# Sums of the softmax by two products with a matrix of ones, in place of transposes and a row sum, in a Hymba encoder block

## The chip, the cores and the metric

The kernel runs on one core of a Trainium2 chip. The metric is the device time in microseconds. The engines are TensorE (PE; PEld is its weight load), VectorE (DVE), ScalarE (ACT), GpSimd (POOL) and SyncE (SP), which issues most of the DMAs. Each engine works through its own instructions in a fixed order and waits on semaphores for the others.

## The reference

One encoder block: 2048 tokens and 16 meta tokens of width 1024, four query heads that share two key/value heads of width 128, four Fourier groups, and an MLP of width 4096, all in float32. The part that the change touches is the softmax of the attention:

```python
h = concat([meta, x])                               # (2064, 1024)
proj = rms_norm(h, g_mix) @ w_in                    # q, k, v, u
q, k = (axial_rope(rms_norm(t, g)) for t, g in ((q, g_q), (k, g_k)))
s = einsum('bkgqd,bksd->bkgqs', q, k) / sqrt(128)
p = softmax(s, axis=-1)
attn = einsum('bkgqs,bksd->bkgqd', p, v)
four = real(fft2(u over tokens and channels)) @ w_f
h = h + concat([rms_norm(attn), rms_norm(four)]) @ w_out
h = h + square(relu(rms_norm(h) @ w_up)) @ w_down
out = rms_norm(h, g_final)[16:]
```

## The kernel before

Products of float32 that have to be exact are taken in two parts: `split` (L67) has ScalarE round a value to float32r, the high part, and VectorE subtract it from the value, the low part; `mm3` (L77) adds three products of such parts. Lines L70/L71 and L80 to L82 are therefore those of many operations, and the tiles' names tell them apart.

The kernel runs in stages: projections with rotary embedding (to about 340 us in the profile), then attention with other work beside it (to about 990 us), then the MLP, by Strassen's scheme with seven products, in two passes over the tokens.

**Attention** (`attention`, L729) runs in 16 units. A unit is 256 query tokens of one key/value group: two heads, so 512 columns. Its keys come in 16 tiles of 128 and one of 96 rows that holds the meta tokens. Scores stand transposed, with keys on the partitions and the 512 query columns along the free dimension:

- `scores` (L759): `mm3` gives a tile of scores in PSUM (tile `s`, two buffers), ScalarE copies it to SBUF (L780), and VectorE keeps a running maximum M over the tiles (L783, L786).
- `stats` (L806): the maximum over all keys of a column has to be taken across partitions. `over_keys` (L790) transposes M in four 128x128 pieces on TensorE (L794) into PSUM and VectorE reduces along the free dimension (L796); `rows_to_cols` (L799) brings the 128x4 result back to a row of 512 on all partitions by four more transposes of a broadcast column (L803). ScalarE copies it to `mb` (L811).
- `softmax` (L813): VectorE subtracts `mb` from two key tiles at once (L840), ScalarE takes the exponential (L841), VectorE adds it to a running sum `acc` (L845, L847), and TensorE multiplies it with V into the PSUM tile `o` (L849). At a unit's last tile VectorE folds `acc` to `sum` (L827, L828), 128x512.
- `finish` (L851), in three steps between which other work may stand: ScalarE copies `o` to SBUF (O, L855); then the sums over the keys, again across partitions: four transposes of `sum` (tile `pm_l`, L794), a reduction (tile `mx_l`, L796) and a reciprocal of 128x4 (L859); then four transposes back (tile `pd_l`, L803) and VectorE's multiplication of O with them, out of PSUM (L861). O is split into `ohl` (one buffer) and stored by SP (L870), or, in the last two units, split straight into the operand `at`. ScalarE squares O (L872), and VectorE adds the squares to `sq` (L876, L879).

The small PSUM tiles of these steps (`pm`, `pd`, and `pys` of the output stage) share one buffer, named "misc".

**What sets the order.** `attention` is a generator, and two others run beside it: `fourier` (tiles `pa`, `py`, `thi`, `C`, `EV`, `UA`) and `out_f` (tiles `yh`, `ysq`, `pof`, `xo`), and after these `out_a` and `flip` (tiles `poa`, `pmt`, `h`). `mix` (L1000) ties the steps of attention to theirs. A unit's finish is put into a list at its last key tile and takes one step at each of the following tiles, while the next unit's scores and exponentials go on; scores run some 20 tiles ahead of the softmax. The language's own scheduler then lays out each engine's instructions in an order of its own, with the buffers that it has, so that a change in one place may move others.

## Time and profile before

| | us |
|---|---|
| median of 3 runs | 2296.43 |
| lowest and highest | 2295.06, 2297.25 |
| profiled execution | 2295.14 |
| its span | 2293.4 |
| TensorE busy, granted clock | 2242.5, 0.994 |
| VectorE busy | 1692.7 |
| ScalarE busy | 1177.4 |
| GpSimd busy | 247.2 |

In the profile's rows a group has its line, engine and operation, the tiles it writes and reads, the shapes and a count; then the busy time in microseconds and the mean of one in nanoseconds; then the idle time before it and what ended that. A row of the timeline begins with the start and the duration in microseconds. A row of stretches has, for each engine, the busy time and the number of instructions between two times, then the granted TensorE clock, the busy share of the DMA engines and their GB/s. Instructions overlap at their ends: an engine starts the next while the last one drains, so the step from start to start is shorter than the duration.

### The profile page before, as it was taken

To read this page: it belongs to the slowest core of one execution; us is meant where nothing else is said; L and a number is where in the kernel's file an instruction comes from. 1 tells how busy PE (TensorE), PEld (TensorE's weight loads), DVE (VectorE), ACT (ScalarE), POOL (GpSimd) and SP (SyncE) were. 2 spreads that over 40 slices of the span, in tenths; PEclk is the share of its full clock that TensorE was granted. 3 is DMA by queue.
4 is the path that set the end of the run, shared out by engine and by line. 5 is a ranking of instruction groups with operands and counts; after the bars stand their busy time and mean duration, and the time that the engine had idled before them with its cause. 6 is when DMAs were issued, how large, how long until landed. Compare 5 with 4: busy or idle time off the path is not lost.

```text
span 2293.4 us, 28136 instructions
## 1 busy us (share of the span) xinstructions
PE 2242.5 (98%) x10238; PEld 1775.1 (77%) x10238; DVE 1692.7 (74%) x2250; ACT 1177.4 (51%) x1997; POOL 247.2 (11%) x285
## 2 busy tenths in 40 slices
PE   9999999999999999999999999999789999899998
PEld 7888986766666666678888878888678888688887
DVE  6435589999998998887776579779555656596795
ACT  6443356656555666677555544334345555443343
POOL 2212120013222022010000010000200000100000
PEclk9999999999999999999999999999899999999999
DMA  6333252133343523366767675543574445764442
GB/s 204 87 105 87 66 164 71 51 120 100 115 137 120 204 87 119 123 262 234 237 227 234 235 276 176 172 129 119 198 302 151 154 149 187 299 201 158 129 138 83
DMA packets 191787, 367.41 MB, mean 160 GB/s; under 512 B 15760, under 2 KB 74768, under 8 KB 189984
## 3 DMA queue, kind: packets, MB, share of 16 engines
q1 hardware_dynamic: 171040, 310.08, 39.9%
q0 software_dynamic: 20464, 55.27, 7.7%
q8 instruction: 80, 1.31, 0.2%
q14 instruction: 59, 0.48, 0.1%
q10 hardware_dynamic: 144, 0.26, 0.0%
HBM read 236.28 MB, written 129.27 MB: 159 GB/s over the span
## 4 chain that ended last, share of the span: by engine, by line
PE 79%; DVE 8%; DMA 6%; ACT 3%; issue 2%; POOL 1%; SPq 1%; POOLq 0%; DVEq 0%; ACTq 0%
PE o L849 6%; PE dx L80 5%; PE dx L82 5%; PE dx L81 5%; PE dy L82 4%; PE dy L80 4%; PE dy L81 4%; PE ux L80 4%; PE ux L81 4%; PE ux L82 4%; PE uy L80 3%; PE uy L82 3%; PE uy L81 3%; PE s L80 2%; PE s L82 2%
## 5 line engine op out<-in xcount | busy, mean ns | idle before, releaser
L70 ACT CAST ah<-a 128x1024 fp32r<-128x1024 f32 x112 | 117.1, 1049 | 259.3 <-PE dx L81 104.9
L849 PE MATMUL o<-S,vn 128*128 128x512 f32 x512 | 243.6, 597 | 4.1 <-ACT S L841 3.4
L80 PE MATMUL dx<-bh,ah 128*128 128x512 f32 x512 | 199.3, 389 | 4.2 <-DVE hs L1485 2.5
L81 PE MATMUL dx<-bl,ah 128*128 128x512 f32 x512 | 199.1, 389 | 1.4 <-DVE bl L71 1.4
L82 PE MATMUL dx<-bh,al 128*128 128x512 f32 x512 | 199.2, 389 | 0.1
L80 PE MATMUL ux<-bf,wuh 128*128 128x512 f32 x448 | 176.8, 395 | 18.8 <-DMA bf<-f_d 18.7
L780 ACT COPY S<-s 128x512 f32<-128x512 f32 x256 | 145.0, 584 | 92.2 <-PE s L82 73.0
L81 PE MATMUL ux<-bf,wuh 128*128 128x512 f32 x448 | 175.8, 392 | 0.0
L82 PE MATMUL ux<-bf,wul 128*128 128x512 f32 x448 | 175.7, 392 | 0.0
L840 DVE TENSOR_TENSOR S<-S,mb 128x1024 f32<-128x1024 f32 x128 | 155.4, 1229 | 11.8 <-ACT mb L811 11.7
L841 ACT ACTIVATE S<-S 128x1024 f32<-128x1024 f32 x128 | 135.1, 1063 | 43.1 <-DVE S L840 41.9
L80 PE MATMUL dy<-bh,ah 128*128 128x512 f32 (+1 forms) x388 | 151.6, 391 | 4.9 <-ACT ah L70 4.9
L71 DVE TENSOR_TENSOR al<-a,ah 128x1024 fp32r<-128x1024 f32 x112 | 136.3, 1222 | 26.6 <-ACT ah L70 26.0
L82 PE MATMUL dy<-bh,al 128*128 128x512 f32 (+1 forms) x388 | 150.8, 390 | 0.7 <-DVE al L71 0.7
L81 PE MATMUL dy<-bl,ah 128*128 128x512 f32 (+1 forms) x388 | 151.3, 390 | 0.0
L849 PEld LDWEIGHTS o<-S,vn 128*128 128x128 f32 x512 | 92.2, 189 | 75.0 <-issue 59.0
L80 PE MATMUL s<-q,kt 128*128 128x512 f32 (+1 forms) x272 | 145.2, 534 | 2.7 <-ACT S L780 2.5
L71 DVE TENSOR_TENSOR bl<-d,bh 128x1024 fp32r<-128x1024 f32 x96 | 117.1, 1220 | 26.7 <-ACT bh L70 26.5
L80 PE MATMUL uy<-bf,wuh 128*128 128x512 f32 x320 | 125.2, 391 | 0.3 <-ACT wuh L70 0.3
L82 PE MATMUL uy<-bf,wul 128*128 128x512 f32 x320 | 124.7, 390 | 0.7 <-DVE wul L71 0.7
L81 PE MATMUL uy<-bf,wuh 128*128 128x512 f32 x320 | 124.9, 390 | 0.0
L786 DVE TENSOR_TENSOR M<-M,S 128x1024 f32<-128x1024 f32 x96 | 117.8, 1227 | 9.1 <-ACT S L780 8.1
(311 smaller groups left out, 5633.5 us busy)
## 6 DMA issues: line engine op xcount, KB each, us to landing
a<-s_d SPq DMA_DIRECT2D x84, 512.0 KB, 3.7
R<-in_w_up_dram SPq DMA_DIRECT2D x32, 1024.0 KB, 5.5
s_d<-s SPq DMA_DIRECT2D x128, 256.0 KB, 2.1
d<-in_w_down_dram SPq DMA_DIRECT2D x52, 512.0 KB, 5.1
s_d<-c SPq DMA_DIRECT2D x96, 256.0 KB, 2.8
f_d<-lf SPq DMA_DIRECT2D x56, 256.0 KB, 2.9
bf<-f_d SPq DMA_DIRECT2D x7, 2048.0 KB, 22.6
a<-s_d POOLq DMA_DIRECT2D x24, 512.0 KB, 5.6
```

The source lines that it names most:

```text
L70: self.high = nc.scalar.copy(hi, src)
L71: self.low = nc.vector.tensor_tensor(lo, src, f32v(hi), op=ALU.subtract)
L80: nc.tensor.matmul(out, a[0], b[0], start=first, stop=False, skip_group_check=chain)
L81: nc.tensor.matmul(out, a[0], b[1], start=False, stop=False, skip_group_check=chain)
L82: nc.tensor.matmul(out, a[1], b[0], start=False, stop=last, skip_group_check=chain)
L780: nc.scalar.copy(S[:, i % 2], ps)
L786: nc.vector.tensor_tensor(M, M, S, op=ALU.max)
L840: nc.vector.tensor_tensor(S, S, mb, op=ALU.subtract)
L841: nc.scalar.activation(p, S, AF.Exp, scale=ISQ)
L849: nc.tensor.matmul(s["O"], v[:, 2 * j % 4 + e], p[:, e], start=i + e == 1, stop=False)
```

## The change

A float32r matrix of ones, 128x128, is made at the start by ScalarE. In `finish`, the `sum` tile (128x512, sums over the keys that lie on a partition) is split into two float32r parts, and two products with the ones add them over the partitions. The result, 128x512 in PSUM, has the column's sum on every partition. VectorE takes the reciprocal of all of it back into `sum`, and multiplies O by that. The transposes, the reduction and the 128x4 tiles of the sums are gone from `finish`; those of the maximum in `stats` stay as they are.

```diff
     ones = const.tile([P, 1], F32, name="ones", tag="ones")
     nc.vector.memset(ones, 1.0)
+    ones_r = const.tile([P, P], R32, name="ones_r")
+    nc.scalar.copy(ones_r, bc(ones, [P, P]))
...
             O = ap2.tile([P, 512], F32, name=f"O_{u}", tag="Osb", bufs=1)
             nc.scalar.copy(O, s["O"])
-            yield
-            sl = over_keys(s["sum"], f"l{u}", ALU.add)
-            rl = ap2.tile([P, 4], F32, name=f"rl_{u}", tag="rl", bufs=2)
-            nc.vector.reciprocal(rl, sl)
-            yield
-            nc.vector.tensor_tensor(O, O, rows_to_cols(rl, f"l{u}"), op=ALU.mult)
+            parts = ap2.tile([P, 2, 512], R32, name=f"sp_{u}", tag="ohl", bufs=1)
+            split(parts[:, 0], parts[:, 1], s["sum"])
+            yield
+            ps = misc(f"pl_{u}")
+            for e in range(2):
+                nc.tensor.matmul(ps, ones_r, parts[:, e], start=e == 0, stop=e == 1)
+            yield
+            nc.vector.reciprocal(s["sum"], ps)
+            nc.vector.tensor_tensor(O, O, s["sum"], op=ALU.mult)
             c = slice(b % 2 * 256, b % 2 * 256 + 256)
```

Line numbers after the change are larger, by two from the new constant on and by five behind `finish`.

The scheduler's new order at the first unit's finish, on VectorE. `M` and `S` with high numbers are the maximum and the scores of the next units, `mb` the maximum of the running one, `acc` its sum. Before:

```order
L783 TENSOR_TENSOR M_4001<-S_0_3929,S_2_3981 128x1024
L796 TENSOR_REDUCE mx_l_3988<-pm_l_3983 128x4
L840 TENSOR_TENSOR S_2_3745<-S_2_3745,mb_3931 128x1024
L859 RECIPROCAL rl_3990<-mx_l_3988 128x4
L786 TENSOR_TENSOR M_4001<-M_4001,S_4_4023 128x1024
L861 TENSOR_TENSOR O_3975<-O_3975,pd_l_4003 128x512
L845 TENSOR_TENSOR acc_3992<-S_0_3734,S_2_3745 128x1024
L71 TENSOR_TENSOR ohl_4009<-O_3975,ohl_4009 128x512
```

And in the changed program, at the same place (`sp` are the two parts, `pl` the product with ones):

```order
L785 TENSOR_TENSOR M_4000<-S_0_3931,S_2_3986 128x1024
L71 TENSOR_TENSOR sp_3979<-sum_3973,sp_3979 128x512
L842 TENSOR_TENSOR S_2_3747<-S_2_3747,mb_3933 128x1024
L865 RECIPROCAL sum_3973<-pl_3988 128x512
L788 TENSOR_TENSOR M_4000<-M_4000,S_4_4018 128x1024
L866 TENSOR_TENSOR O_3977<-O_3977,sum_3973 128x512
L847 TENSOR_TENSOR acc_3991<-S_0_3736,S_2_3747 128x1024
L71 TENSOR_TENSOR ohl_4004<-O_3977,ohl_4004 128x512
```

The split's low part stands where the reduction stood, the wide reciprocal where the narrow one did, and the rest is as it was; in front of the maximum, the running sum and the multiplication there is now the reciprocal of 512 columns.

On TensorE, around the same finish (`pa` belongs to the Fourier work, `o_3727` and then `o_3993` are this unit's and the next one's products with V). Before:

```order
L567 MATMUL pa_1_4087<-cw_342,EV 128x128 x4
L794 MATMUL pm_l_3983<-ident,sum_3971 128x128 x4
L829 MATMUL o_3727<-ph_16_3968,vm_3584 128x512
L567 MATMUL pa_2_4096<-cw_342,EV 128x128 x4
L567 MATMUL pa_3_4105<-cw_342,EV 128x128
L849 MATMUL o_3993<-S_0_3734,vn_0_3576 128x512 x2
L803 MATMUL pd_l_4003<-ident,rl_3990 128x128 x4
L567 MATMUL pa_3_4105<-cw_342,EV 128x128 x2
L849 MATMUL o_3993<-S_2_3745,vn_0_3576 128x512 x2
```

And in the changed program:

```order
L831 MATMUL o_3729<-ph_16_3970,vm_3586 128x512
L569 MATMUL pa_2_4091<-cw_344,EV 128x128
L863 MATMUL pl_3988<-sp_3979,ones_r 128x512
L569 MATMUL pa_2_4091<-cw_344,EV 128x128
L569 MATMUL pa_3_4100<-cw_344,EV 128x128 x2
L851 MATMUL o_3992<-S_0_3736,vn_0_3578 128x512
L863 MATMUL pl_3988<-sp_3979,ones_r 128x512
L851 MATMUL o_3992<-S_0_3736,vn_0_3578 128x512
```

The two groups of four transposes are gone; the first product with ones follows the unit's last product with V, and the second, which needs the low part, comes four rows later, between two products with V of the next unit.

## The prediction

> **What bounds the kernel now.** I read the page first (its head, its table of busy time, the slices, the chain's shares), then the busy times of the attention stage in three stretches, then the timeline around single finishes.

> ```profile
> span 2293.4 us, 28136 instructions
> PE 2242.5 (98%) x10238; PEld 1775.1 (77%) x10238; DVE 1692.7 (74%) x2250; ACT 1177.4 (51%) x1997; POOL 247.2 (11%) x285
> DVE  6435589999998998887776579779555656596795
> PE 79%; DVE 8%; DMA 6%; ACT 3%; issue 2%; POOL 1%; SPq 1%; POOLq 0%; DVEq 0%; ACTq 0%
> ```

> Over the whole span TensorE sets the time: 98% busy, 79% of the chain. But the 74% of VectorE is a mean over unlike stages. Its digits stand at 8 and 9 from the sixth slice to the eighteenth (57 us each), and that is attention. The stretches, and behind the dots the same three for the reciprocal alone:

> ```profile
> core 0: us, PE busy (x) PEld busy (x) DVE busy (x) ACT busy (x) POOL busy (x), PEclk, DMA share, GB/s
> 380.00:620.00 240.00, 235.26 (x1030) 161.34 (x1029) 235.39 (x288) 149.26 (x251) 44.27 (x42) 1.00 0.29 90
> 620.00:820.00 200.00, 199.41 (x783) 137.88 (x782) 181.55 (x229) 116.58 (x196) 42.41 (x42) 1.00 0.43 144
> 820.00:990.00 170.00, 167.30 (x672) 112.49 (x671) 144.22 (x182) 106.89 (x175) 32.91 (x23) 1.00 0.35 115
> ...
> 380.00:620.00 240.00, 1.01 (x6) 1.00 0.29 90
> 620.00:820.00 200.00, 0.84 (x5) 1.00 0.43 144
> 820.00:990.00 170.00, 0.87 (x5) 1.00 0.35 115
> ```

> Its counts (x6, x5, x5) tell how many of the 16 units finish in each stretch. In the first, VectorE works 235.39 of 240 us and so has 4.6 us left; in the second 18.5, in the third 25.8. TensorE is as dense there. So the stage has two engines at their limit, VectorE above all in its first 240 us, and both sides of the change have to be priced: what TensorE is spared and what VectorE is given.

> **What TensorE is spared.**

> ```profile
> 379.65 0.39 PE L81 MATMUL s<-q,kt 128*128 128x512 f32 x1
> 379.88 0.40 PE L82 MATMUL s<-q,kt 128*128 128x512 f32 x1
> 381.45 0.60 PE L794 MATMUL pm_l<-ident,sum 128*128 128x128 f32 x4
> 385.05 0.60 PE L803 MATMUL pd_l<-ident,rl 128*128 128x128 f32 x4
> ```

> Matmuls overlap, so what one costs is its step from start to start, not its duration. A score product of 128x512 follows the last after 379.88 - 379.65 = 0.23 us. Four transposes last 0.60 us together, of which the last alone is 0.27, so a step is (0.60 - 0.27) / 3 = 0.11. A finish loses 8 x 0.11 = 0.88 us and gains two products of the scores' shape and type, 0.46: 0.42 us less, 6.7 us over 16 units. That is the whole gain on TensorE, 0.3% of the span. The transposes of the maximum (pm_m, pd_m) stay.

> **What VectorE and ScalarE are given.** The words of the change name a row sum that VectorE loses. It gets the low part of the split in its place, of the same width, and its reciprocal grows from 128x4 to 128x512, since the sums now stand on all partitions.

> ```profile
> L859 DVE RECIPROCAL rl<-mx_l 128x4 f32<-128x4 f32 x16 | 2.7, 170 | 0.0
> L796 DVE TENSOR_REDUCE mx_l<-pm_l 128x4 f32<-128x512 f32 x16 | 10.9, 683 | 0.2 <-PE pm_l L794 0.2
> L71 DVE TENSOR_TENSOR ohl<-O,ohl 128x512 fp32r<-128x512 f32 x14 | 9.6, 687 | 0.2 <-ACT ohl L70 0.2
> L861 DVE TENSOR_TENSOR O<-O,pd_l 128x512 f32<-128x512 f32 x16 | 10.9, 681 | 1.1 <-PE pd_l L803 0.9
> L70 ACT CAST ohl<-O 128x512 fp32r<-128x512 f32 x14 | 8.7, 619 | 6.0 <-DVE O L861 6.0
> ```

> The new low part (the shape of L71) costs what the reduction did, 0.69 against 0.68 us: they cancel. The multiplication stays, with one operand now from SBUF and no longer from PSUM; L71 there, all from SBUF, lasts as long. ScalarE gets one cast of 0.62 us in each unit, 9.9 in all; it is busy 149 of 240 us in the tightest stretch, so as work this is hidden.

> What is left is the reciprocal, whose width of 512 no row shows. Here again the step counts:

> ```profile
> 384.40 0.17 DVE L859 RECIPROCAL rl<-mx_l 128x4 f32<-128x4 f32 x1
> 384.49 1.20 DVE L786 TENSOR_TENSOR M<-M,S 128x1024 f32<-128x1024 f32 x1
> ...
> 420.54 0.17 DVE L859 RECIPROCAL rl<-mx_l 128x4 f32<-128x4 f32 x1
> 420.62 1.20 DVE L783 TENSOR_TENSOR M<-S,S 128x1024 f32<-128x1024 f32 x1
> ...
> 422.88 0.68 DVE L861 TENSOR_TENSOR O<-O,pd_l 128x512 f32<-128x512 f32 x1
> 423.48 1.22 DVE L786 TENSOR_TENSOR M<-M,S 128x1024 f32<-128x1024 f32 x1
> 424.62 0.69 DVE L71 TENSOR_TENSOR ohl<-O,ohl 128x512 fp32r<-128x512 f32 x1
> ...
> 785.58 0.15 DVE L1045 COPY ass<-pas 128x4 f32<-128x4 f32 x1
> 785.65 1.40 DVE L74 SCALAR_TENSOR_TENSOR wol<-wor,cols,woh 128x512 fp32r<-128x512 f32 x2
> ```

> 512 elements step 0.60 us, 1024 step 1.14: 1.05 ns for an element and 0.06 us for the instruction. The copy of four elements fits that (0.07). The reciprocal of four elements doesn't: its successor starts after 0.09 and 0.08 us, 0.085 in the mean, 0.025 over the 0.06. Spread over four elements that is 6 ns each, six times an ordinary element. At width 512: 0.06 + 512 x 0.006 = 3.1 us.

> The ends: if what exceeds is a fixed delay of this operation, 512 elements cost what any other operation of that width does, 0.60. If 0.09 is the true reading, 0.03 over four elements is 7.5 ns, and the instruction costs 3.9. I take 3.1, since the rows show the operation itself to be slow and the excess grows with nothing else that I can name; four elements read to 0.01 us are a weak lever, so I keep both ends.

> [...]

> Per unit, then, VectorE pays 3.1 - 0.085 = 3.0 us more, 48 us over the stage.

> **What of it is on the path.** First stretch: 235.4 + 6 x 3.0 = 253.4 us of work where 240 stood. What VectorE idles there now, 4.6 us, are short waits for ScalarE and TensorE, which a longer queue doesn't remove; I leave them: 258, or **+18**. TensorE's six savings are lost in it, since it now waits. Second: 181.6 + 15 = 196.6 of 200, or 98.3% busy, as full as the first stretch is today (98.1%), and that one kept TensorE at 98%: it fits. Third: 144.2 + 15 = 159.2 of 170: it fits. In these two TensorE keeps its savings, 10 x 0.42 = **-4**. But the reciprocal is one block in an in-order queue: the subtraction, the running sum and the maximum of the next unit stand behind it for 3 us, and so do ScalarE's exponentials, which wait for the subtraction.

> ```profile
> ACT S L780 <- PE s L82: 63.5, 51, 4.6
> ACT ohl L70 <- DVE O L861: 6.0, 4, 2.2
> ```

> ScalarE now waits for O at its cast to ohl in four finishes of 16, up to 2.2 us. With O 3 us later it will wait at most of them, and behind that cast stand the copies (L780) that free the two PSUM buffers of the scores. ScalarE has time to make up for it (it idles 63.5 us for scores), the two buffers have not. TensorE's own new wait, of its second product for the low part, takes the place of its transposes' waits for the sum and for the reciprocal; the next unit's products with V stand behind it. For all of this I put half a microsecond on each of the ten finishes: **+5**.

> Last unit, in the same timeline:

> ```profile
> 986.61 0.66 PE L794 MATMUL pm_l<-ident,sum 128*128 128x128 f32 x4 [0.30 <-DVE sum L828]
> 989.08 0.69 DVE L861 TENSOR_TENSOR O<-O,pd_l 128x512 f32<-128x512 f32 x1 [0.88 <-PE pd_l L803]
> 992.70 0.89 DVE L879 TENSOR_TENSOR sq<-sq,O 128x256 f32<-128x256 f32 x2 [0.71 <-ACT O L872]
> 994.41 0.97 PEld L1042 LDWEIGHTS pas<-ones,sq 128*128 128x128 f32 x8
> ```

> From the sum to the multiplication it takes 989.08 - 986.61 = 2.5 us; then a cast of 0.62, a subtraction of 0.69, products of 0.5 and a reciprocal of 3.1, 4.9: 2.4 later. The squares end at 993.6 and the next block's product with them starts at 994.41, so 0.8 us of it is covered: **+2**.

> At no cost: the cast to ones_r at the start. ScalarE's table load ends near 2.0 us and it waits for x until 4.31, where 0.3 us of a 128x128 cast finds room; its price without that cover is that 0.3.

> ```profile
> 0.74 1.28 ACT L259 ACT_TABLE_LOAD   x1 [0.74 <-PEq L1709]
> 4.31 0.60 ACT L259 ACTIVATE jk<-x 128x512 f32<-128x512 f32 x1 [2.29 <-DMA x<-in_x_dram]
> ```

> Also the parts' use of the ohl buffer (its last store was issued a whole unit, some 38 us, earlier), and the stores of o_d that SP now issues behind some weight loads: what reads them comes several units later. The loads of keys and values on POOL change places with additions of squares, on an engine busy 11% of the span.

> Sum: 18 - 4 + 5 + 2 = +21 us on the profiled execution's 2295.14 (its span is 2293.4; 1.7 lie around it). That execution is 1.3 below the median of 2296.43, so I forecast **2316**.

> **The rivals.** *The reciprocal streams like any other operation* (0.60 us). Then VectorE pays 0.5 us a unit. The first stretch takes 235.4 + 3.1 = 238.5 of its 240 us and loses something between 0 and the 3.1, say 1, TensorE saves 4 in the others, the last unit is even (0.62 + 0.69 + 0.5 + 0.6 = 2.4): 2295 - 3 = 2292. For it: the instruction after the short reciprocal lasts 1.20 and not 1.22, so part of the delay may be handed back. Against it: the step of 0.085. It decides up to about 0.085 + 4.6 / 6 = 0.85 us for a reciprocal; above that the first stretch overflows. This is the case that is not slower.

> *Slower still* (3.9 us, 3.8 more a unit): first stretch 235.4 + 22.9 + 4.6 = 263, +23; second 200.5 of 200 with its short waits, +4; blocks and last unit +10; savings -2: +35, 2330. For it: the reading 0.09.

> *The slack is shared out.* VectorE's total from 380 to 990 is 561 us, with 48 more 609 of 610. Attention steps are tied to the steps of the Fourier and output work beside them, but each engine's order is laid out anew, so work beside attention can slip from the first stretch into the later ones. Perfectly shared, only the last unit's +2 remains: 2297. Against it: none of the three stretches now runs VectorE over 98.1%.

> **How the numbers follow.** The forecast's case 0.52 (its own range 2305 to 2326), the slower one 0.20, the streaming one 0.18, the shared slack 0.10. This kernel's measurement can tell about 0.2%, 4.6 us, from no change. Slower: 0.52 + 0.20 = 0.72. The streaming case lies at the edge of that bound: 0.10 of it within, 0.08 faster; with the shared slack, 0.20 within. The range takes in the ends of the reciprocal: 2291 to 2334.

> **What would show it.** In the changed kernel's groups, the row of the reciprocal: near 3.1 us each, 50 us in all, or 0.7. VectorE's busy share from 380 to 620 at 98% or more with fewer units finished in it, and TensorE's below 95%, waiting for VectorE's subtraction through ScalarE's exponential. ScalarE's wait for O at ohl in most finishes. If the reciprocal is short and the time still grows, the order laid out anew is the cause, not the price; if it is long and the time doesn't grow, the slack was shared.

## The result, and the profile after

| | before | after |
|---|---|---|
| median of 4 runs each, taken in turn, us | 2296.81 | 2321.81 |
| lowest and highest | 2295.06, 2297.25 | 2318.47, 2327.26 |
| ratio, 95% interval | | 1.0113 [1.0092, 1.0133] |
| profiled execution, its span | 2295.14, 2293.4 | 2327.26, 2325.5 |

The changed kernel is 25 us slower. The profiled execution is the slowest of its four: its mean granted TensorE clock was 0.988, while the fastest, 2318.47, had 0.993. Positions below are read from it, sizes from the ratios of medians. Of all executions told of here one ran in a slow state: of the kernel with the new finish in units 6 to 15, 3777.61 us at a granted clock of 0.556, which counts in that kernel's median and not in its ratio.

From the page after: its table of busy time, the slices of VectorE, and the shares of the chain:

```profile
PE 2256.7 (97%) x10142; PEld 1774.0 (76%) x10142; DVE 1740.1 (75%) x2250; ACT 1188.4 (51%) x2014; POOL 236.3 (10%) x285
DVE  5434579999999989988676769679645646597796
PE 47%; DMA 3%; DVE 2%; ACT 1%; issue 1%; SPq 0%; POOLq 0%; POOL 0%; DVEq 0%; ACTq 0%
```

The page's chain says little here: the shares that it names add up to 54%, and its 15 longest pieces all begin behind 1062 us, so it doesn't reach into attention. VectorE's digits do: from the seventh slice to the nineteenth, 58 us each, they stand at 8 and 9, where before it was the sixth to the eighteenth. The stretches of after, with the one behind attention (columns as in the prediction: busy time and count on PE, PEld, DVE, ACT and POOL, then the granted clock, the DMA share, GB/s):

```profile
380.00:620.00 240.00, 225.22 (x926) 150.01 (x925) 232.08 (x262) 141.52 (x235) 29.36 (x38) 0.97 0.27 83
620.00:820.00 200.00, 198.47 (x758) 133.35 (x757) 196.55 (x229) 117.86 (x201) 46.91 (x44) 1.00 0.45 147
820.00:990.00 170.00, 164.61 (x636) 110.28 (x635) 155.97 (x180) 108.05 (x177) 27.82 (x22) 0.99 0.33 109
990.00:1060.00 70.00, 63.52 (x274) 46.52 (x272) 56.33 (x74) 45.68 (x73) 11.60 (x8) 0.95 0.59 226
```

and the last of them before:

```profile
990.00:1060.00 70.00, 68.27 (x339) 55.85 (x338) 56.27 (x71) 55.11 (x87) 7.23 (x6) 1.00 0.77 287
```

In the first 240 us VectorE is as busy as it was (232 against 235) but gets through 262 instructions where it had 288, and TensorE, 104 instructions short, is idle for 14.8 us where it was idle for 4.7. Six finishes fall into this stretch in both kernels; with two products in place of eight transposes they account for 36 of the 104. In the second stretch both are full. In the last TensorE loses another 4.8 us of busy time, and what it does there it does at a clock of 0.95.

Where the reciprocals start gives the delay along the way. The sixth finish, the last one, and the first product of the MLP, from the timeline of before and then of after:

```profile
582.12 0.16 DVE L859 RECIPROCAL rl<-mx_l 128x4 f32<-128x4 f32 x1
988.03 0.18 DVE L859 RECIPROCAL rl<-mx_l 128x4 f32<-128x4 f32 x1
1035.19 0.48 PE L80 MATMUL ux<-bf,wuh 128*128 128x512 f32 x1
```

```profile
601.49 3.34 DVE L865 RECIPROCAL sum<-pl 128x512 f32<-128x512 f32 x1
1013.30 3.36 DVE L865 RECIPROCAL sum<-pl 128x512 f32<-128x512 f32 x1 [0.59 <-PE pl L863]
1064.54 0.50 PE L80 MATMUL ux<-bf,wuh 128*128 128x512 f32 x1
```

The reciprocal starts 19.4 us late at the sixth finish and 25.3 at the last; in between it goes up and down (28.2 at the twelfth, 21.2 at the fifteenth). Its own 3 us come on top of these: the last multiplication of O starts at 1017.15 us against 989.08, 28.1 late, and the MLP 29.4 late.

What a late VectorE does to TensorE shows at the fourth finish. From the timelines of VectorE, ScalarE and TensorE of after, in brackets the idle time before and its releaser:

```profile
510.31 3.35 DVE L865 RECIPROCAL sum<-pl 128x512 f32<-128x512 f32 x1
513.57 1.16 DVE L788 TENSOR_TENSOR M<-M,S 128x1024 f32<-128x1024 f32 x1
514.65 0.94 DVE L866 TENSOR_TENSOR O<-O,sum 128x512 f32<-128x512 f32 x1
515.51 1.21 DVE L847 TENSOR_TENSOR acc<-S,S 128x1024 f32<-128x1024 f32 x1
...
515.70 0.62 ACT L70 CAST ohl<-O 128x512 fp32r<-128x512 f32 x1 [1.14 <-DVE O L866]
516.76 1.08 ACT L782 COPY S<-s 128x512 f32<-128x512 f32 x2 [0.44 <-DVE acc L847]
...
517.40 0.50 PE L80 MATMUL s<-q,kt 128*128 128x512 f32 x1 [2.42 <-ACT S L782]
```

The reciprocal holds the maximum, the multiplication and the running sum back; ScalarE waits for the multiplication (1.14 us) and then for the running sum, which has to have read an S buffer before a score can be copied into it (0.44); TensorE waits 2.42 us for that copy, since both of its score buffers in PSUM are full, as the two copies in a row (x2) show.

### The profile page after: what moved, and what is told of

It is laid out like the page before. It is cut to its first block, busy times and chain, and to the rows that moved or that the text cites. A ratio compares the mean times of both kernels' runs of the same rounds, so it can differ in the third digit from the quotient of the medians.

```text
span 2325.5 us, 27983 instructions
## 1 busy us (share of the span) xinstructions
PE 2256.7 (97%) x10142; PEld 1774.0 (76%) x10142; DVE 1740.1 (75%) x2250; ACT 1188.4 (51%) x2014; POOL 236.3 (10%) x285
## 4 chain that ended last, share of the span: by engine, by line
PE 47%; DMA 3%; DVE 2%; ACT 1%; issue 1%; SPq 0%; POOLq 0%; POOL 0%; DVEq 0%; ACTq 0%
PE dx L81 5%; PE dx L80 5%; PE dx L82 5%; PE ux L80 4%; PE ux L81 4%; PE ux L82 4%; PE dy L82 4%; PE dy L80 4%; PE dy L81 4%; PE uy L80 3%; PE uy L82 3%; PE uy L81 3%; DMA bf<-f_d 1%; DMA lf<-m_d 1%; DMA d<-in_w_down_dram 0%
## 5 line engine op out<-in xcount | busy, mean ns | idle before, releaser
L70 ACT CAST ah<-a 128x1024 fp32r<-128x1024 f32 x112 | 117.1, 1049 | 264.2 <-PE dx L81 106.7
L81 PE MATMUL dx<-bl,ah 128*128 128x512 f32 x512 | 199.6, 390 | 2.0 <-DVE bl L71 2.0
L82 PE MATMUL dx<-bh,al 128*128 128x512 f32 x512 | 199.4, 389 | 0.1
L81 PE MATMUL ux<-bf,wuh 128*128 128x512 f32 x448 | 176.0, 393 | 0.0
L82 PE MATMUL ux<-bf,wul 128*128 128x512 f32 x448 | 176.0, 393 | 0.0
L71 DVE TENSOR_TENSOR al<-a,ah 128x1024 fp32r<-128x1024 f32 x112 | 136.0, 1219 | 28.7 <-ACT ah L70 28.1
L81 PE MATMUL dy<-bl,ah 128*128 128x512 f32 (+1 forms) x388 | 151.7, 391 | 0.0
L82 PE MATMUL dy<-bh,al 128*128 128x512 f32 (+1 forms) x388 | 151.2, 391 | 0.2 <-DVE al L71 0.2
L80 PE MATMUL s<-q,kt 128*128 128x512 f32 (+1 forms) x272 | 135.8, 499 | 13.5 <-ACT S L782 13.2
L71 DVE TENSOR_TENSOR bl<-d,bh 128x1024 fp32r<-128x1024 f32 x96 | 116.8, 1218 | 25.2 <-ACT bh L70 25.0
L81 PE MATMUL uy<-bf,wuh 128*128 128x512 f32 x320 | 124.7, 390 | 0.0
L1217 ACT ACTIVATE c<-c 128x512 f32<-128x512 f32 x96 | 60.5, 632 | 125.4 <-DVE c L1262 122.5
L82 PE MATMUL uy<-bf,wul 128*128 128x512 f32 x320 | 124.4, 389 | 0.0
```

The lines of the kernel that those rows point to most:

```text
L70: self.high = nc.scalar.copy(hi, src)
L71: self.low = nc.vector.tensor_tensor(lo, src, f32v(hi), op=ALU.subtract)
L80: nc.tensor.matmul(out, a[0], b[0], start=first, stop=False, skip_group_check=chain)
L81: nc.tensor.matmul(out, a[0], b[1], start=False, stop=False, skip_group_check=chain)
L82: nc.tensor.matmul(out, a[1], b[0], start=False, stop=last, skip_group_check=chain)
L1217: nc.scalar.activation(dst, src, AF.Relu)
```

## The experiments

Where a run goes by a change in what stands before, its diff is against the changed kernel, else it is said. us are medians; the ratio is to the kernel before, run on the same chip in turn. In the expectations V is the theory that VectorE's price sets the loss, O the rival that names something else.

**The price taken away, and doubled.**

```diff
-            nc.vector.reciprocal(s["sum"], ps)
+            nc.vector.tensor_copy(s["sum"], ps)
```

> The changed kernel, with the reciprocal left out: VectorE copies the sums from PSUM in its place, 128x512 like it, so O is multiplied by the sums; splits, products with ones, waits and buffers stay. Theory V (VectorE's queue is full and the 3.35 us of the wide reciprocal overflow it): a copy steps about 0.6 us, VectorE pays 0.5 us a unit over the kernel before, so nearly the whole loss goes: 2289 to 2299 us. Theory O (the loss comes from the new waits for cast and low part, and from the order laid out anew): those stay, so 2312 to 2325 us.

2298.81 us, ratio 1.0013 [1.0004, 1.0022]. With a short instruction in the reciprocal's place, and everything else of the change kept (products, split, order of the steps; only the division is left out), some 22 us of the 25 are gone. O falls as the main cause. What is left does not arise in attention: in this kernel's profile the last multiplication of O starts at 984.85 us, 4.2 earlier than before, which is in line with TensorE's saving, and the MLP at 1036.29, 1.1 later. Behind attention TensorE waits 2.49 and 3.07 us for ScalarE, and the last stretch is at 0.95, as in after:

```profile
990.00:1060.00 70.00, 64.30 (x297) 51.64 (x296) 50.69 (x64) 49.82 (x76) 15.22 (x6) 0.95 0.68 253
```

```diff
             nc.vector.reciprocal(s["sum"], ps)
+            nc.vector.reciprocal(s["sum"], ps)
```

> The changed kernel with the reciprocal taken twice from the same PSUM tile; nothing else. V: another 16 x 3.27 = 52 us in a stage where VectorE has little left (640.9 of 680 us busy between 380 and 1060): 2360 to 2378 us. O: the price of the instruction matters little, 2322 to 2335 us.

2383.11 us, 1.0387 [1.0371, 1.0403]: 61 us above the change for 16 x 3.26 = 52 us of work. V's range was 5 us too low, O falls. The second reciprocal costs more than itself. The clock can be a part of that: in this kernel's profile the stretches from 380, 620 and 820 us have granted clocks of 0.95, 0.99 and 0.97, where after's have 0.97, 1.00 and 0.99. Over 240, 200 and 170 us that is an estimated 19 us of full clock lost against 9. The rows of the three kernels, after, copied and doubled (there the second of the two reciprocals):

```profile
L865 DVE RECIPROCAL sum<-pl 128x512 f32<-128x512 f32 x16 | 53.6, 3348 | 0.9 <-PE pl L863 0.8
```

```profile
L865 DVE COPY sum<-pl 128x512 f32<-128x512 f32 x16 | 10.9, 682 | 0.9 <-PE pl L863 0.8
```

```profile
L866 DVE RECIPROCAL sum<-pl 128x512 f32<-128x512 f32 x16 | 53.5, 3342 | 0.0
```

**The price without the products.** Against the kernel before: its transposes and row sum stay, and the reciprocal is taken behind the transposes back, 512 wide.

```diff
-            rl = ap2.tile([P, 4], F32, name=f"rl_{u}", tag="rl", bufs=2)
-            nc.vector.reciprocal(rl, sl)
             yield
-            nc.vector.tensor_tensor(O, O, rows_to_cols(rl, f"l{u}"), op=ALU.mult)
+            nc.vector.reciprocal(s["sum"], rows_to_cols(sl, f"l{u}"))
+            nc.vector.tensor_tensor(O, O, s["sum"], op=ALU.mult)
```

> The kernel before, with its eight transposes and its row sum, but with the sums brought back to the 512 columns first and the reciprocal taken there, 128x512 out of PSUM: no products with ones, no split. V: the loss comes whole, without TensorE's saving: 2318 to 2332 us. O: no new wait for cast or low part, so near the kernel before, 2296 to 2304 us.

2325.92 us, 1.0132 [1.0118, 1.0146]. With the old transposes the wide reciprocal costs as much as with the new products. V holds, O falls: the products are not what costs.

**In which units.** The changed finish for units 0 to 5, for 6 to 15, and for all but the last; the finish of before in the others:

```diff
+            if u < 6:
                 parts = ap2.tile([P, 2, 512], R32, name=f"sp_{u}", tag="ohl", bufs=1)
...
+            else:
+                yield
+                sl = over_keys(s["sum"], f"l{u}", ALU.add)
...
```

> The new finish (split, products with ones, wide reciprocal) in the first six units alone; the other ten finish as before. V with the forecast's sum by stretches: the first stretch alone overflows, +17 to +21 us, the later stretches and the last unit as before: 2312 to 2318 us, with the sixth finish at about 601 us of the profile. If the loss were spread evenly over the finishes (O), six of sixteen would cost 9 to 10 us: 2304 to 2306 us.

2309.87 us, 1.0056 [1.0040, 1.0071], 12.9 us: below V's range, above O's. The timeline and the last stretches show why V was high:

```profile
599.55 3.34 DVE L866 RECIPROCAL sum<-pl 128x512 f32<-128x512 f32 x1
639.83 0.15 DVE L872 RECIPROCAL rl<-mx_l 128x4 f32<-128x4 f32 x1
...
1002.48 0.18 DVE L872 RECIPROCAL rl<-mx_l 128x4 f32<-128x4 f32 x1
1049.63 0.48 PE L80 MATMUL ux<-bf,wuh 128*128 128x512 f32 x1
```

The sixth finish is 17.4 us late and the seventh 18.2 (621.6 before), but the last one 14.5: with short reciprocals again, some 4 us are made good behind the first stretch, most of it by the eighth finish (680.88 against 666.22 us, 14.7 late).

> The reverse: the first six units finish as before, the last ten by the new way. V: VectorE has 18.5 and 25.8 us left there, which holds 10 x 3.26: 0 to +4 us for the ten finishes and up to +8 us at the end, where TensorE stood 4.8 us for VectorE: 2297 to 2307 us. O, even spread: 2310 to 2313 us.

With `u >= 6`: 2307.14 us, 1.0046 [1.0034, 1.0059], 10.6 us. At the upper edge of V's range; O falls. The fifteenth multiplication of O starts at 968.36 us, 2.5 late, the last at 996.13, 7.0 late, the MLP at 1042.88, 7.7 late. So nine of these ten units cost 2.5 us in this profile, and the last one most of the rest, within its own finish.

> The changed kernel, but the last unit finishes as before; it stands at the handover to the MLP, where the changed kernel's distance to the one before grew from 21 us at the last but one finish to 29 us at the first product of the MLP. V: the long chain of the last finish (2.4 us more) is what TensorE stands for there, so 2 to 7 us come back: 2314 to 2320 us. O: it is the order laid out anew, so the handover stays as it is, 2320 to 2324 us.

With `u < 15`: 2315.42 us, 1.0084 [1.0069, 1.0099], 19.3 us. V's range holds; the last unit alone costs 6.6 of the 25.9 us that after's ratio gives. That it is the longer chain alone is not shown, since the order behind it changes too. TensorE's longest wait behind attention and its stretch, of this kernel:

```profile
PE poa L80 <- DVE h L1070: 1.2, 1, 1.2
```

```profile
990.00:1060.00 70.00, 67.07 (x316) 50.16 (x315) 61.29 (x81) 52.82 (x83) 6.57 (x8) 1.00 0.65 246
```

In after that wait is 4.8 us long and the clock 0.95. The copied kernel, with a short chain, has its waits of 2.49 and 3.07 us and the same clock there, though for another instruction.

**Work or block.** Is it the 3.3 us in sum, or that they stand in one piece? The reciprocal in four pieces of 128 columns:

```diff
-            nc.vector.reciprocal(s["sum"], ps)
+            for h in range(4):
+                nc.vector.reciprocal(s["sum"][:, h * P:(h + 1) * P], ps[:, h * P:(h + 1) * P])
```

> The changed kernel with its reciprocal in four pieces of 128 columns, between which the scheduler may put other work: the same number of elements, no long block. V, by work: the same 3.3 us and three more starts of 0.06, 2320 to 2328 us. If the block is what hurts (5 us of the forecast): 2313 to 2318 us.

2326.12 us, 1.0133 [1.0116, 1.0151], in the work theory's range. But it doesn't decide: the scheduler put the four side by side,

```profile
385.07 3.39 DVE L866 RECIPROCAL sum<-pl 128x128 f32<-128x128 f32 x4 [0.16 <-PE pl L863]
388.38 1.16 DVE L788 TENSOR_TENSOR M<-M,S 128x1024 f32<-128x1024 f32 x1
```

so the block was as long as ever. (It shows the price: 0.83 us a piece from start to start.) So the pieces were put into steps of their own:

```diff
             for h in range(4):
                 nc.vector.reciprocal(s["sum"][:, h * P:(h + 1) * P], ps[:, h * P:(h + 1) * P])
+                if h < 3:
+                    yield
```

> The changed kernel with the reciprocal in four pieces of 128 columns and a key tile's other work allowed between them: in the order on VectorE no more than two pieces now stand side by side (in the run with four pieces without this they all stood side by side, so that the block stayed 3.4 us). Work theory (V): it is the sum of 3.3 us a unit in a full queue that costs, not the length of the block: 2320 to 2328, sixth finish's last piece ending at 602 to 608 us, as the reciprocal does now (604.8). Block theory (O): what stands behind a block of 3.3 us for the next unit (subtraction, maximum, running sum) sets much of the loss; with blocks of 0.9 to 1.7 us TensorE's stands of over 1.6 us and its half clock go: 2308 to 2317, and no granted clock under 0.99 in the stretch from 380 to 620 us (0.97 with the change).

2322.87 us, 1.0110 [1.0093, 1.0127]. Now other work does stand between them; the sixth finish in VectorE's timeline, then the first stretch:

```profile
600.06 1.75 DVE L866 RECIPROCAL sum<-pl 128x128 f32<-128x128 f32 x2
601.74 1.15 DVE L788 TENSOR_TENSOR M<-M,S 128x1024 f32<-128x1024 f32 x1
...
606.09 0.93 DVE L866 RECIPROCAL sum<-pl 128x128 f32<-128x128 f32 x1
...
380.00:620.00 240.00, 226.19 (x934) 149.38 (x933) 232.43 (x281) 142.19 (x239) 30.32 (x38) 0.99 0.26 83
```

Half of what the block theory foresaw came: the clock in the first stretch is 0.99 again. The time did not follow: the sixth finish's last piece ends at 607.0 us, where the work theory had 602 to 608, TensorE's busy time there is 226.19 us against 225.22, and the ratio is after's. So no gain from shorter blocks is shown. They are not free of another cost, though: the steps between the pieces put the multiplication of O off (608.03 us at the sixth finish, 605.03 in after), and a gain may be hidden by that. That the sum of the work sets the loss rests on the copied and the doubled kernel.

**A row sum taken off VectorE, without the wide reciprocal.** Against the kernel before: four products of 128x128 pieces of `sum` with the column of ones give the 128x4 sums; the narrow reciprocal and the transposes back stay.

```diff
-            sl = over_keys(s["sum"], f"l{u}", ALU.add)
+            ps = misc(f"pl_{u}", (P, 4))
+            for a in range(4):
+                nc.tensor.matmul(ps[:, a:a + 1], s["sum"][:, a * P:(a + 1) * P], ones, start=True, stop=True)
...
-            nc.vector.reciprocal(rl, sl)
+            nc.vector.reciprocal(rl, ps)
```

> The kernel before, with the four transposes of the sums and VectorE's row sum replaced by four products of a 128x128 piece of the sums with a column of ones, so that the sums come as 128x4 at once; narrow reciprocal and the four transposes back stay. TensorE loads the same four pieces; VectorE loses 0.60 us a unit and gains nothing. V: VectorE is a bound in the first stretch, so 16 x 0.6 = 9.6 us less of its work gives 1 to 8 us: 2288 to 2295 us. O: no difference that can be told, 2294 to 2299 us.

2300.36 us, 1.0020 [1.0011, 1.0029]: both theories missed. VectorE has less to do, and the seventh finish comes at 618.1 us in place of 621.6, but from 800 us on it is lost again, and more (last finish 990.3 against 988.0). The same in the first six units only, and in the first ten:

> The kernel before, with the sums of the first six finishes taken by four products of 128x128 pieces of sum with the column of ones (128x4 in PSUM, no row sum, narrow reciprocal, transposes back as before), the last ten as before. If VectorE's queue in the first stretch is what bounds (V), the row sum of 0.6 us that goes from six finishes brings its seventh finish to 616 to 619 us (621.6 before) and, with the later finishes as they were, 2 to 4 us are kept: 2291 to 2295. If the order laid out anew decides more than a row sum (O), as in the run with such sums in all sixteen, the gain is lost behind 800 us: 2296 to 2301.

> The same with the first ten finishes of the new kind (column products), the last six as before. V: the seventh finish at 616 to 619 us as with six, nothing more from the four that follow, where VectorE has time: 2291 to 2295. O: somewhere from 2292 to 2301, and not where the run with six lies, by over 2 us.

2294.77 us, 0.9992 [0.9983, 1.0001], and 2295.82 us, 0.9999 [0.9990, 1.0007]. The first median lies at V's upper end and the second just above it, but neither can be told from the kernel before, so no gain is shown. O, which had 2296 or more for the first and over 2 us between the two, missed as well. The seventh finish was at 619.1 us with ten, close to what V had, but at 623.95 with six, although the first six finishes are of the same kind in both; where these part is shown in the last section. So an edit of this stage can cost some 5 us by the order and the waits that come with it, as the column sums in all units did, and a row sum less is worth no more than that. No version beat the kernel before.

## Why the prediction was right, and which terms were wrong

The forecast of 2316 is 6 us below the measured 2321.81, in its own case's range and with its sign. (Its 21 us were added to the profiled execution; on the median of before, 2296.43, they give 2317.) Step by step:

- **The reciprocal's price** was right, from 0.025 us of excess over four elements. The step from the reciprocal at 510.31 to the next instruction at 513.57 is 3.26 us, (3.26 - 0.06) / 512 = 6.25 ns an element against 6 forecast, and 3.1 us was taken. That it came so close is partly luck: the two readings of the step, 0.08 and 0.09 us, stand for 5 and 7.5 ns. Over the whole run VectorE works 47.4 us more (1740.1 against 1692.7), 48 forecast. The streaming rival falls with the same row; put in by hand (the copy) it gives 2299, where that rival had 2292.
- **The first stretch, +18**, was right as a place and a mechanism: 19.4 us late at the sixth finish, 17.4 where only these units were changed. VectorE is busy for 96.7%, not the 98% forecast: it idles 7.9 us and not 4.6. TensorE's 93.8% is under the 95% named. But it does not wait through the exponential, as the sign said (3.9 us for it from 380 to 1065 us, 3.4 before); it waits for the score copies, as the rows below show. But as a share of the total it was too large: changed alone, the first six cost 12.9 us. The step that failed is that a delay there is kept to the end; the slack behind it gives some 4 us back as long as it is there.
- **The ten others, +5 and -4**, were too small. Nine of them (units 6 to 14) cost 19.3 - 12.9 = 6.4 us where 9 x (0.5 - 0.42) = 0.7 was put. "It fits" was true of VectorE's work (196.55 us measured in the second stretch, 196.6 forecast), but at 98% that stretch no longer makes good what the first one loses: without a loss in front of them the same nine units cost 2.5 us (the fifteenth multiplication, in the run of units 6 to 15). That the half microsecond is the block's is not borne out: with blocks of half the length nothing was gained. ScalarE's wait for O at its cast came in 5 finishes, not in most.

```profile
ACT ohl L70 <- DVE O L866: 8.6, 5, 3.2
...
PE s L80 <- ACT S L782: 12.6, 7, 3.4
PE poa L80 <- DVE h L1062: 6.0, 2, 4.8
```

```profile
PE s L80 <- ACT S L780: 2.1, 6, 0.6
```

(Waits of after, then of before, from 380 to 1065 us: in all, times, longest.) What grew is TensorE's wait for the score copies, 12.6 us in 7 times, where before it was 2.1 in 6.

- **The last unit, +2**, was the term furthest off: 6.6 us. Two things were missed. Its own chain grew by more than the 2.4 us counted: from the last fold of the sums to the multiplication it takes 7.1 us against 3.2 (to 989.08), 3.9 more, with `h` of the output stage between the reciprocal and the multiplication. And what comes behind was not counted. The timeline of before and then of after there:

```profile
985.89 0.67 DVE L828 TENSOR_TENSOR sum<-sum,S 16x512 f32<-16x512 f32 x1
```

```profile
1010.03 0.68 DVE L830 TENSOR_TENSOR sum<-sum,S 16x512 f32<-16x512 f32 x1
...
1017.15 0.68 DVE L866 TENSOR_TENSOR O<-O,sum 128x512 f32<-128x512 f32 x1
...
1020.98 4.34 POOL L194 TENSOR_TENSOR rs_m<-ms_m,mhalf 128x1 f32<-128x1 f32 x1 [9.51 <-DVE ms_m L192]
...
1025.35 1.15 ACT L1074 ACTIVATE h<-h,rs_m 128x1024 f32<-128x1024 f32 x1 [4.22 <-POOL rs_m L194]
1027.47 1.23 DVE L71 TENSOR_TENSOR wul<-us,wuh 128x1024 fp32r<-128x1024 f32 x1 [2.49 <-ACT wuh L70]
1028.61 0.16 DVE L192 TENSOR_SCALAR ms_a<-ass 128x4 f32<-128x4 f32 x1
...
1031.67 0.80 PE L80 MATMUL poa<-woh,at 128*128 128x512 f32 x1 [4.78 <-DVE h L1062]
1032.26 0.63 PE L81 MATMUL poa<-wol,at 128*128 128x512 f32 x1
```

The squares are late (the last at 1023.36 us, 992.70 for their pair before); the small mean behind them (`ms_a`) stands in VectorE's queue behind a subtraction that waits 2.49 us for ScalarE, although its input lay ready from about 1025; GpSimd and VectorE's `h` follow, and TensorE stands for 4.8 us. Then its products take 0.63 us in place of 0.39. ScalarE in its turn had waited 4.22 us for GpSimd's `rs_m`, which took 4.34 us there and 0.55 at the same place where the last unit finished as before. In the copied kernel one such instruction took 9.34 us, and that is the wait of its handover. In both traces it ended 0.3 to 0.4 us after an unbroken run of VectorE's operations did (1025.32 after 1024.98 us, 1030.34 after 1029.93); why it is long is not shown. So it is open whether a part of the 6.6 us hangs on what runs beside GpSimd in the order laid out anew, and not on the price alone.

- **The slack shared out** (2297) falls: nothing of the first stretch's work was moved to the later ones beyond the 4 us above, and the later ones filled up with their own.

The terms measured, 12.9 + 6.4 + 6.6 = 25.9, against 18, 0.7 and 2: one too large, two too small, and part of the error cancelled, which is luck. That they add up says nothing, since each is the difference to the one before. Measured the other way round, the last ten units alone cost 10.6 us and not 13.0. Each ratio is known to 3 to 5 us either side, and their differences, the last two terms, less well; that the last unit costs more than 2 is borne out by the 3.9 us of its chain and by TensorE's wait behind it, 4.8 us against 1.2.

## What to carry to other kernels

A reduction that leaves its result on all partitions makes whatever is done to the result as wide as the operand: look up what that operation costs for each element (6.25 ns here) before its narrow form is widened, from the step between starts if only a narrow one is there to read (0.085 us for 128x4, 3.26 for 128x512). Here the cost added to VectorE, with 4.6 us of idle time in its stretch of 240, was paid nearly in full there, 19.4 us late for 6 x (3.26 - 0.085) = 19.1 of work, but behind it some 4 us were made good where short reciprocals followed, so price the stretches together and not each alone. At a handover between stages follow the late result to the engine that waits for it, through whatever stands in the queues between.

## What the hardware showed that was not expected

```profile
832.40:835.82 3.42, 0.32 (x2) 0.00 (x0) 1.56 (x2) 1.42 (x2) 1.97 (x1) 1.00 0.00 0
835.82:839.23 3.41, 3.16 (x7) 2.49 (x8) 1.73 (x2) 2.59 (x4) 0.00 (x0) 0.51 0.00 0
```

Here a window in which TensorE is busy for 0.32 us is followed by one at half clock. The same place in the two kernels with column sums in the first six units and in the first ten, and the window behind it:

```profile
516.91:520.32 3.41, 1.06 (x4) 0.48 (x3) 1.44 (x2) 2.17 (x3) 1.20 (x2) 0.99 0.32 101
520.32:523.73 3.41, 3.41 (x6) 1.55 (x5) 3.41 (x4) 0.51 (x2) 0.00 (x0) 0.51 0.22 71
```

```profile
516.00:519.41 3.41, 2.13 (x8) 1.26 (x8) 2.50 (x3) 2.25 (x3) 2.19 (x2) 1.00 0.29 96
519.41:522.82 3.41, 3.41 (x14) 2.14 (x13) 3.41 (x4) 1.95 (x5) 0.00 (x0) 1.00 0.45 135
```

In the first TensorE waits 2.35 us for an exponential and then runs at half clock, in the second 1.28 and doesn't; the next finish comes at 541.46 and 538.92 us, 2.5 apart: 1.07 by the wait, and half speed for 3.41 us accounts for up to 1.7. In after's trace from 380 to 1065 us the windows in front of the five stretches have TensorE idle for 2.97, 2.39, 1.75, 3.14 and 3.41 us, and no other window at full clock for more than 1.42; before has none over 1.06 there. From 380 us to the end of both traces all 14 windows at full clock with 1.75 us or more were followed by one at half clock, and none of those with less (the longest 1.73). In the traces of the experiments, from 380 to 1065 us, the edge is less sharp: of the windows between 1.6 and 1.9 us some were followed so, and one of those with less (1.2 us). A window already at half clock was followed by a second with less idle time: 1.11 and 1.25 us in the two longer stretches of after's five.

In these traces half clock goes with the idle time inside one window, and not with the length of the wait, as the fourth finish shows. In after the wait of 2.42 us shown above (514.97 to 517.40) lies in one window but for 0.03 us, and the next is at half clock. With the last unit finished as before, the same wait is as long:

```profile
519.06 0.50 PE L80 MATMUL s<-q,kt 128*128 128x512 f32 x1 [2.43 <-ACT S L782]
```

but there the grid parts it into 1.01 and 1.42 us, and the clock stays; this kernel's stretch from 380 to 620 us has 0.98, after's 0.97. The clock stays, too, behind two waits of 2.80 us in the MLP: from 1986.74 to 1989.54 us in before, parted into 1.59 and 1.21, and from 2019.14 to 2021.94 us in after, parted into 1.14 and 1.66. So a wait of 2.4 us came with a half-clock window in one execution and with none in another, by where the grid lay, and such a window of 3.41 us can by estimate cost up to 1.7 us more than the wait itself. The spread of after's four executions goes with the clock: 2327.26 us at 0.988, 2322.36 and 2321.26 at 0.990, 2318.47 at 0.993.

How much of the loss is the clock's? In the profiled execution 24 us at half speed bound it at 12. The fastest execution of after had 0.993, 0.001 below the profiled one of before, which is worth some 2 us over its span, and a few at most with the rounding; it was still 23.3 us slower (2318.47 against 2295.14). So most of the loss is there without the clock.
